# Projections of a two-layer attention trunk: float32r high and low parts replaced by float16 parts with measured power-of-two scales

## The chip, the cores and the metric

The kernel runs on one core of one Trainium2 chip. The metric is the device time of one execution in microseconds (us), given as a median over runs. A core has a matrix engine (PE, with PEld for its loading of stationary tiles), a vector engine (DVE), a scalar engine (ACT), GpSimd (POOL) and SyncE (SP), which in this kernel issues all DMA transfers. Each engine works through a queue of its own in order.

## The reference

A trunk of two layers over 1024 tokens of width 1024, 16 heads of 64. Each layer is a gated mixer:

```python
for i in range(DEPTH):                       # DEPTH = 2
    h = rms_norm(x, norm_g[i])
    if i % 2 == 0: o, gate = fox_mixer(h, ...)            # layer 1
    else:          o, gate = dsw_mixer(h, cos, sin, ...)  # layer 2
    x = x + (o * jax.nn.silu(gate)) @ w_out
# fox_mixer: proj = h @ w_in                       # 4*1024 + 16 columns
#   q, k = rms_norm(per head) * gain;  v, gate, f_logit = the rest
#   c = cumsum(log_sigmoid(f_logit + b_f))
#   o = softmax(q k^T / 8 + c_i - c_j, causal) v
# dsw_mixer: proj = h @ w_in                       # 9*1024 + 1024 columns
#   three groups (window, dilation) = (128,1), (512,4), (2048,16):
#   q, k = partial_rotary(rms_norm(per head) * gain); banded softmax; v
#   o = the three groups' outputs weighted by softmax over their lse
# rms_norm(x, g) = x * rsqrt(mean(x*x) + 1e-6) * g,  all float32
```

## The kernel before, in words

**Precision by pairs.** Each projection is computed from a high and a low part of both operands: `xh`, `xl` for the activations and two halves of `w` for the weights, all float32r. A product takes three matmuls: xh·wh, xh·wl, xl·wh.

**Tiling.** Weights come in blocks of up to 384 columns. `project` (L308, its matmul L313) computes one block for one tile of 128 tokens: eight steps over the contraction, each with three matmuls whose stationary operand is a 128x128 piece of xh or xl and whose moving operand is a slab of the weight. There are 38 such blocks of eight tiles: three for the gates of layer 1 (384, 272 and 384 columns; the middle one carries the forget logits), eight for layer 1's heads, three for the gates of layer 2 (384, 256, 384) and 24 for layer 2 (eight head pairs by three dilation groups). 36 of them have 384 columns. `project_t` (L318, matmul L336) is the output projection at the end of each layer, with the weight stationary and 512 tokens moving.

**Order.** PE is pinned to program order; the order of the other engines is made by a scheduler, from the order in which the program issues its work and from priorities, and each engine then keeps its own order. The program issues work through `Flow`: a slot passes for every six projection matmuls (`flow.tick()` in `project`), so 32 slots to a block, and `flow.at(slot, fn)` puts a piece of work at a slot. While PE does block n, `Weights.ahead` (L294) prepares block n+1 at slots of the table `CFG`:

- `load` (L248): four pairs of slabs, 128x2x384 float32, into two rotating `raw` buffers, at slots 0, 4, 13, 20.
- `bound` (L255, DVE reduce at L258): the largest absolute value of the v columns, for blocks of layer heads only, at slots 9, 14, 22, 27. `scale` (L262) makes from it a power of two for v, at slot 28.
- `split` (L283): for each of eight slabs a copy to float32r on ACT (L289), and the residue by a subtraction (L291), six on POOL and two on DVE.

**Activations.** In layer 1 x arrives transposed from memory (`split_xt`, L521): it is multiplied by the norm's gain and split. It is not divided by the norm; the per-token factor `rx` (L538, `row_factor`) is applied to the results instead, in the gates, in the head norms' epsilon and in v. At the end of layer 1, `grown` (L775) adds the output projection to x, writes x and x times the gain to memory, and gathers squares; `take` (L816) reloads and splits x for layer 2 (L825, L826), and `sums` makes the factors `rx2`. Layer 2's dilated tiles reload x from memory in `reload_x`.

**Around the projections.** In layer 1 (the FoX stage) the scores of head pair n are computed while block n+1 projects. Probabilities are split into float16 halves (`p_transpose`: ACT copy, a subtraction on POOL at L498), transposed by DMA into `ptt`, and multiplied with v at L506 to L508. q and k are transposed by DMA into `qk_t`. Layer 2 (the dilated stage) does likewise with its own subtraction at L912. At the end, `transpose_rows` (L343) turns the gated output y on PE and splits it into xh, xl for `project_t`.

The lines around a split in the program before:

```python
nc.scalar.copy(w[:, 0, :n], raw[:, k % 2, :n])
eng = nc.vector if own or (cfg["wl"][self.layer] >> k) & 1 else nc.gpsimd
eng.tensor_sub(w[:, 1, :n], raw[:, k % 2, :n], w[:, 0, :n].bitcast(F32))
```

Of the kernel before, what the change touches and what calls it, by code (L numbers as in the profile page):

```python
# [82 lines left out]
def trunk(ctx, tc, ins, out, cfg):  # L83
# [42 lines left out]
    ss_d = dram.tile([S], F32, name="ss_d")  # L126
# [16 lines left out]
    xh = const.tile([P, KT, S], F32R, name="xh")  # L143
    xl = const.tile([P, KT, S], F32R, name="xl")
# [81 lines left out]
    gmax = const.tile([P, 2], F32, name="gmax")  # L226

    gmax2 = const.tile([P, 2], F32, name="gmax2")
# [4 lines left out]


# [3 lines left out]
    class Weights:  # L238


        def __init__(self, src, n, vcols=None, layer=0):
            self.src, self.n, self.vcols, self.layer = src, n, vcols, layer
            self.raw, self.slabs, self.vs = {}, [], None
            if vcols is not None:
                self.vm = sm.tile([P, KT // 2], F32, name="vm", tag="vm")
                self.vm2 = sm.tile([P, KT // 2], F32R, name="vm2", tag="vm2")

        def load(self, i, tag=None):  # L248
            if tag is None:
                self.raw[i] = w_p.tile([P, 2, 384], F32, name="raw", tag="raw", bufs=2)  # L250
            else:
                self.raw[i] = lay([P, 2, 384], F32, name="raw", tag=tag)
            nc.sync.dma_start(self.raw[i][:, :, : self.n], self.src[:, 2 * i : 2 * i + 2, :])

        def bound(self, i):  # L255
            if self.vcols is None:
                return
            nc.vector.tensor_reduce(self.vm[:, i : i + 1], self.raw[i][:, :, self.vcols], AX.XY, ALU.max, apply_absolute_value=True)  # L258
            if i == KT // 2 - 1:
                nc.vector.tensor_mul(self.vm2, self.vm, self.vm)  # L260

        def scale(self):  # L262

            if self.vcols is None:
                return

            ws = under["ps"][:, 384 : 384 + KT // 2]
            nc.tensor.matmul(ws, ones, self.vm2, start=True, stop=True)  # L270
            v1 = sm.tile([P, 1], F32, name="v1", tag="v1")
            nc.vector.tensor_reduce(v1, ws, AX.X, ALU.add)
            nc.vector.tensor_scalar(v1, v1, gmax2[:, self.layer : self.layer + 1], None, ALU.mult)

            e = v1.bitcast(I32)
            nc.vector.tensor_scalar(e, e, 1, 0x7FC00000, ALU.logical_shift_right, ALU.bitwise_and)
            nc.vector.tensor_scalar(e, e, float(127 << 22), None, ALU.add)
            nc.vector.tensor_single_scalar(e, e, 0x7F800000, ALU.bitwise_and)
            nc.vector.tensor_scalar(e, e, float(125 << 23), float(154 << 23), ALU.max, ALU.min)
            self.vs = sm.tile([P, 1], F32, name="vs", tag="vs")  # L280
            nc.vector.tensor_scalar(self.vs.bitcast(I32), e, -1.0, float(267 << 23), ALU.mult, ALU.add)

        def split(self, k, own=False):  # L283
            raw, n = self.raw[k // 2], self.n
            if "w2" in layer["bufs"] and k >= KT - 2:
                w = lay([P, 2, 384], F32R, name="w2", tag="w2")
            else:
                w = w_p.tile([P, 2, 384], F32R, name="w", tag="w", bufs=cfg["wbufs"])
            nc.scalar.copy(w[:, 0, :n], raw[:, k % 2, :n])  # L289
            eng = nc.vector if own or (cfg["wl"][self.layer] >> k) & 1 else nc.gpsimd  # L290
            eng.tensor_sub(w[:, 1, :n], raw[:, k % 2, :n], w[:, 0, :n].bitcast(F32))  # L291
            self.slabs.append(w)

        def ahead(self):  # L294

            s0 = flow.now
            for i in range(KT // 2):
                flow.at(s0 + cfg["wload"][i], lambda i=i: self.load(i))
                flow.at(s0 + cfg["wbound"][i], lambda i=i: self.bound(i))
            flow.at(s0 + cfg["wscale"], self.scale)  # L300
            for k in range(KT):
                flow.at(s0 + cfg["wsplit"][k], lambda k=k: self.split(k))
            return self

    def part(src, i, layer=0):
        return Weights(src[i], src[i].shape[2], None, layer)

    def project(w, cols):  # L308
        n = w.n
        ps = under["ps"] = ps_pj.tile([P, 512], F32, name="pj", tag="pj")  # L310
        for k in range(KT):
            for i, (a, j) in enumerate(((xh, 0), (xh, 1), (xl, 0))):
                nc.tensor.matmul(ps[:, :n], a[:, k, cols], w.slabs[k][:, j, :n], start=(k == 0 and i == 0), stop=(k == KT - 1 and i == 2))  # L313
# [4 lines left out]
    def project_t(h, w, done):  # L318


        n = w.n // P
# [8 lines left out]
        for i, (b, m, k) in enumerate(todo):  # L330
# [4 lines left out]
            for x, (j, a) in enumerate(((0, xh), (0, xl), (1, xh))):  # L335
                nc.tensor.matmul(ps[m], w.slabs[k][:, j, m * P : (m + 1) * P], a[:, k, 512 * b : 512 * (b + 1)], start=(k == 0 and x == 0), stop=(k == KT - 1 and x == 2))  # L336
# [6 lines left out]
    def transpose_rows(row, k0, n, t):  # L343
# [4 lines left out]
        dh = xh[:, k0 : k0 + n, t * P : (t + 1) * P]  # L348
        with tc.high_priority(cfg["ph_"]):
            nc.scalar.copy(dh, pv)  # L350
            nc.vector.tensor_sub(xl[:, k0 : k0 + n, t * P : (t + 1) * P], pv, dh.bitcast(F32))
# [9 lines left out]
    def load_gbc(layer):  # L361
        gbc = lay([P, D], F32, name="gbc", tag="ph")
        nc.sync.dma_start(gbc, norm_g[layer].partition_broadcast(P))
        gm = gmax[:, layer : layer + 1]
# [746 lines left out]
```

## Time and profile before

| what | value |
|---|---|
| median of 3 runs | 1812.54 us (1809.61 to 1814.23) |
| span of the profiled execution | 1816.7 us |
| PE busy | 1737.0 us, 96% |
| DVE, ACT, POOL busy | 60%, 56%, 54% |
| DMA traffic | 290.79 MB |

The profiled execution is one of its own, and its span, 1816.7 us, is the only time it has; it lies about 4 us above the median of the timed runs. A matmul's row gives its own duration, and durations overlap: the pace of PE is the distance between starts. The stages by time: first gates to about 143 us, FoX heads to about 600, output projection to about 662, second gates to about 750, dilated heads to about 1720, last output projection to the end.

### The profile page before, as it was taken

How to read it: one execution, taken by the hardware profiler on the slowest of the kernel's cores; microseconds unless marked ns; L12 is line 12 of the kernel's file. 1: busy time of each engine (PE TensorE's matmuls, PEld its weight loads, DVE VectorE, ACT ScalarE, POOL GpSimd, SP SyncE). 2: the span in 40 equal slices, each digit the busy share in tenths (PEclk: the TensorE clock that was granted, in tenths of full speed). 3: DMA queues.
4: the chain of work that ended last, by engine and by line, in shares of the span. 5: the costliest groups of instructions: out<-in, count | busy, mean ns of one | idle time of the engine just before them, and what ended most of it. 6: DMA issues, size and time to landing. Idle time of an engine off the chain costs nothing.

```text
span 1816.7 us, 38150 instructions
## 1 busy us (share of the span) xinstructions
PE 1737.0 (96%) x13276; PEld 1641.7 (90%) x13276; DVE 1093.3 (60%) x3674; ACT 1011.0 (56%) x2696; POOL 973.5 (54%) x1175
## 2 busy tenths in 40 slices
PE   7999999999988989999999999999999999999999
PEld 6999888888876779999999989999999999999877
DVE  8546666666664453365556585666675666667631
ACT  6536666666665465455555665555555555555620
POOL 4215565556545431255656566667576666757530
PEclk9999999999999999999999999999999999999999
DMA  8447999999999763456767687667677776667852
GB/s 285 127 130 140 193 190 185 176 177 183 187 190 207 213 188 114 127 113 134 142 133 144 146 191 143 157 140 152 138 163 144 162 151 143 149 140 179 189 154 85
DMA packets 653189, 290.79 MB, mean 160 GB/s; under 512 B 512306, under 2 KB 616754, under 8 KB 652996
## 3 DMA queue, kind: packets, MB, share of 16 engines
q1 hardware_dynamic: 652996, 288.36, 71.4%
q8 instruction: 104, 1.70, 0.4%
q14 instruction: 89, 0.73, 0.1%
HBM read 126.46 MB, written 37.03 MB: 90 GB/s over the span
## 4 chain that ended last, share of the span: by engine, by line
PE 45%; DMA 12%; DVE 6%; ACT 4%; issue 3%; POOL 3%; SPq 1%; DVEq 0%; POOLq 0%; ACTq 0%
PE pj L313 33%; PE pj L336 7%; DMA raw<-in_w_dsw 5%; PE s L450 2%; DMA qk_t<-hl 2%; DMA ptt<-ph 2%; DMA og_d<-og 1%; POOL hl L425 1%; POOL w L291 1%; DMA cmb<-og_d 1%; DVE w L291 1%; DVE hl L426 1%; DVE u L422 1%; PE ob L506 1%; DVE p L906 1%
## 5 line engine op out<-in xcount | busy, mean ns | idle before, releaser
L313 PE MATMUL pj<-w,xh 128*128 128x384 f32 (+2 forms) x4864 | 1259.6, 341 | 30.2 <-ACT w L289 7.3
L313 PEld LDWEIGHTS pj<-w,xh 128*128 128x128 f32 x4864 | 873.1, 191 | 38.9 <-DVE ge L481 7.8
L313 PE MATMUL pj<-w,xl 128*128 128x384 f32 (+2 forms) x2432 | 817.6, 336 | 0.2 <-DVE xl L530 0.2
L313 PEld LDWEIGHTS pj<-w,xl 128*128 128x128 f32 x2432 | 464.7, 191 | 0.9 <-DVE xl L530 0.9
L291 POOL TENSOR_TENSOR w<-raw,w 128x384 fp32r<-128x384 f32 (+2 forms) x258 | 261.7, 1035 | 233.3 <-ACT w L289 228.8
L498 POOL TENSOR_TENSOR ph<-p,ph 128x512 f16<-128x512 f32 (+3 forms) x176 | 172.9, 999 | 161.9 <-ACT ph L495 160.7
L289 ACT CAST w<-raw 128x384 fp32r<-128x384 f32 (+2 forms) x352 | 162.6, 501 | 114.8 <-PE pj L336 37.4
L425 POOL TENSOR_TENSOR hl<-u,hl 128x512 f16<-128x512 f32 x128 | 151.2, 1181 | 125.0 <-ACT hl L424 124.9
L912 POOL TENSOR_TENSOR ph<-p,ph 128x768 f16<-128x768 f32 (+2 forms) x96 | 155.3, 1618 | 102.9 <-ACT ph L911 102.9
L383 ACT ACTIVATE sq<-pj 128x256 f32<-128x256 f32 x256 | 97.2, 380 | 168.9 <-DVE u L378 167.2
L450 PE MATMUL s<-qk_t 128*128 128x128 f16 (+1 forms) x1504 | 162.0, 248 | 19.2 <-DVE acc L658 10.4
L336 PE MATMUL pj<-xh,w 128*128 128x512 f32 x512 | 170.4, 404 | 2.2 <-ACT p L907 1.1
L258 DVE TENSOR_REDUCE vm<-raw 128x1 f32<-128x256 f32 x128 | 53.6, 419 | 156.2 <-DMA raw<-in_w_dsw 118.6
L506 PEld LDWEIGHTS <-ptt 128*128 128x128 f16 x1136 | 102.9, 98 | 48.8 <-issue 27.5
L389 DVE SCALAR_TENSOR_TENSOR vt<-pj,vsr,vt 128x128 f16<-128x128 f32 x256 | 89.6, 350 | 93.2 <-ACT vt L388 92.8
L450 PEld LDWEIGHTS <-qk_t 128*128 128x128 f16 x1504 | 110.2, 98 | 36.1 <-issue 22.0
L424 ACT CAST hl<-u 128x512 f16<-128x512 f32 x128 | 79.2, 619 | 104.9 <-DVE u L422 88.6
L495 ACT CAST ph<-p 128x512 f16<-128x512 f32 (+3 forms) x176 | 88.9, 537 | 72.7 <-DMA ptt<-ph 72.3
L492 ACT ACTIVATE p<-p,acc 128x512 f32<-128x512 f32 (+2 forms) x192 | 109.0, 609 | 30.6 <-DVE acc L658 27.4
L336 PEld LDWEIGHTS pj<-xh,w 128*128 128x128 f32 x512 | 97.6, 191 | 24.5 <-DVE xr L779 1.5
L378 DVE TENSOR_TENSOR u<-pj,gr 128x256 f32<-128x256 f32 x256 | 106.4, 416 | 18.4 <-PE pj L313 18.3
L907 ACT ACTIVATE p<-p,og 128x128 f32<-128x128 f32 (+1 forms) x256 | 98.1, 441 | 33.6 <-DVE og L906 33.4
(171 smaller groups left out, 2609.4 us busy)
## 6 DMA issues: line engine op xcount, KB each, us to landing
raw<-in_w_dsw SPq DMA_DIRECT2D x96, 384.0 KB, 3.7
raw<-in_w_fox SPq DMA_DIRECT2D x32, 384.0 KB, 3.7
og_d<-og SPq DMA_DIRECT2D x64, 132.0 KB, 3.2
cmb<-og_d SPq DMA_DIRECT2D x64, 132.0 KB, 3.3
bc<-c_d SPq DMA_DIRECT2D x32, 256.0 KB, 3.9
gs_d<-ge SPq DMA_DIRECT2D x32, 192.0 KB, 3.2
xt<-in_xt SPq DMA_DIRECT2D x16, 256.0 KB, 6.1
xrow<-in_x SPq DMA_DIRECT2D x8, 512.0 KB, 6.3
```

Source lines behind the costliest of these rows:

```text
L289: nc.scalar.copy(w[:, 0, :n], raw[:, k % 2, :n])
L291: eng.tensor_sub(w[:, 1, :n], raw[:, k % 2, :n], w[:, 0, :n].bitcast(F32))
L313: nc.tensor.matmul(ps[:, :n], a[:, k, cols], w.slabs[k][:, j, :n], start=(k == 0 and i == 0), stop=(k == KT - 1 and i == 2))
L336: nc.tensor.matmul(ps[m], w.slabs[k][:, j, m * P : (m + 1) * P], a[:, k, 512 * b : 512 * (b + 1)], start=(k == 0 and x == 0), stop=(k == K ...
L378: nc.vector.tensor_mul(u[:, t % 2].rearrange("p (a b) d -> p a b d", a=2), ps[:, : 4 * HD].rearrange("p (a b d) -> p a b d", a=2, b=2), gr ...
L425: nc.gpsimd.tensor_sub(hl[:, :, :4, 1], u, hl[:, :, :4, 0])
L450: nc.tensor.matmul(s[:, c0 : c0 + cnt * P].rearrange("p (c s) -> p c s", c=cnt), qk[:, i, blk], kk[:, j : j + cnt, e], start=(h == 0), sto ...
L492: nc.scalar.activation(p, p, AF.Exp, bias=acc, scale=-1.0)
L498: (nc.gpsimd if pool_l else nc.vector).tensor_sub(ph[:, e, 1, cols], p, ph[:, e, 0, cols])
L506: nc.tensor.matmul(o[:, e, :], hi, vt[:, j, e, HD:], start=(b == 0), stop=False, skip_group_check=True)
L907: nc.scalar.activation(p[:, e], p[:, e], AF.Exp, bias=acc[:, e : e + 1], scale=-1.0)
L912: nc.gpsimd.tensor_sub(ph[:, 1], st["p"], ph[:, 0])
```

## The change

All operands of the projections become float16. So that high and low parts keep their accuracy in float16's range, everything is scaled by powers of two which are found from the data:

- `bound` reduces **all** columns of **every** block (768 elements a pair instead of 256), at slots 8, 10, 12, 15. `scale`, at slot 20, now runs for every block: the squares are summed over partitions by a matmul with ones (`spread_sums`), and the power of two `sw`, the inverse `inv` and, for head blocks, the scaled epsilon, the column factor and v's factor follow in 9 or 13 small DVE operations.
- `split` works on a pair of slabs and comes after `scale`, at slots 21, 23, 25, 27. Pairs 1 and 3: ACT copies with `scale=sw`, and one DVE instruction multiplies and subtracts 768 elements (L301). Pairs 0 and 2: POOL multiplies `raw` in place (L303), ACT copies, POOL subtracts (L305).
- Because nothing can be split before the whole block is measured, `raw` has four buffers instead of two; the loads are at slots 2, 4, 6, 9.
- x is divided by its norm before the split. In layer 1 a diagonal matrix `dg` of the row factors goes through a matmul with ones (L578, `nb`), and DVE multiplies x by it. For layer 2 `factors` does the same with 512 tokens at a time, `take` multiplies, splits and writes the normalised x to `xm_d`, which `reload_x` reads. The factors `rx`, `rx2` and `vsr` at the results are gone; the constants `inv`, `eps` and `vs` of the block are applied in the same instructions.
- y has its own `yh`, `yl` with a scale `sy`, from the largest gate value (a reduction a gate tile into `peak`) and the smallest weight scale.
- At the start, row 0, x tile 0, all four weight pairs and the gains are loaded before anything is split.

```diff
-    xh = const.tile([P, KT, S], F32R, name="xh")
-    xl = const.tile([P, KT, S], F32R, name="xl")
+    xh, xl, yh, yl = (const.tile([P, KT, S], F16, name=n) for n in ("xh", "xl", "yh", "yl"))
...
+    def spread_sums(src, n):
...
+        nc.tensor.matmul(ws, ones.bitcast(src.dtype), src, start=True, stop=True)
+        v1 = sm.tile([P, 1], F32, name="v1", tag="v1")
+        nc.vector.tensor_reduce(v1, ws, AX.X, ALU.add)
+        return v1
...
-            self.raw[i] = w_p.tile([P, 2, 384], F32, name="raw", tag="raw", bufs=2)
+        def load(self, i):
+            self.raw[i] = w_p.tile([P, 2, 384], F32, name="raw", tag="raw", bufs=4)
...
-            nc.vector.tensor_reduce(self.vm[:, i : i + 1], self.raw[i][:, :, self.vcols], AX.XY, ALU.max, apply_absolute_value=True)
+            nc.vector.tensor_reduce(self.vm[:, i : i + 1], self.raw[i][:, :, : self.n], AX.XY, ALU.max, apply_absolute_value=True)
...
+        def split(self, i, own=False):
+            raw, n = self.raw[i][:, :, : self.n], self.n
+            w = self.pairs[i] = w_p.tile([P, 2, 2, 384], F16, name="w", tag="w", bufs=cfg["wbufs"])
+            if own or (cfg["wl"][self.layer] >> i) & 1:
+                nc.scalar.activation(w[:, 0, :, :n], raw, AF.Copy, scale=self.sw)
+                nc.vector.scalar_tensor_tensor(w[:, 1, :, :n], raw, self.sw, w[:, 0, :, :n], ALU.mult, ALU.subtract)
             else:
+                nc.gpsimd.tensor_scalar(raw, raw, self.sw, None, ALU.mult)
+                nc.scalar.copy(w[:, 0, :, :n], raw)
+                nc.gpsimd.tensor_sub(w[:, 1, :, :n], raw, w[:, 0, :, :n])
...
+    def split_xt(t):
+        nb = ps_s.tile([P, 512], F32, name="nb", tag="s")
+        nc.tensor.matmul(nb[:, :P], ones.bitcast(F32), fac.pop(t), start=True, stop=True)
+        for h in range(2):
+            xv = xts.pop((t, h)).rearrange("p (k s) -> p k s", k=4)
+            nc.vector.tensor_mul(xv, xv, nb[:, :P].unsqueeze(1).broadcast_to([P, 4, P]))
+            dh = xh[:, 4 * h : 4 * h + 4, t * P : (t + 1) * P]
+            nc.scalar.copy(dh, xv)
+            (nc.gpsimd if t > 1 and h else nc.vector).tensor_sub(xl[:, 4 * h : 4 * h + 4, t * P : (t + 1) * P], xv, dh)
...
         def split(i):
+            nc.vector.tensor_mul(xs[:, i], xs[:, i], fac2[b])
...
-CFG = dict(... wl=(0x50, 0x50), ... wbufs=12, ... wload=(0, 4, 13, 20), wbound=(9, 14, 22, 27), wscale=28, wsplit=(10, 11, 15, 16, 29, 29, 30, 30))
+CFG = dict(... wl=(0xA, 0xA), ... wbufs=8, ... wload=(2, 4, 6, 9), wbound=(8, 10, 12, 15), wscale=20, wsplit=(21, 23, 25, 27))
```

**Where instructions move.** First the start of PE's queue. Before, PE begins with the projection of tile 0, slab by slab (pj is the result, w the weight pair, the number behind a name the buffer's):

```order
L313 MATMUL pj_217<-w_149,xh_107 128x384 x2
L313 MATMUL pj_217<-w_149,xl_108 128x384
L313 MATMUL pj_217<-w_152,xh_107 128x384 x2
L313 MATMUL pj_217<-w_152,xl_108 128x384
L313 MATMUL pj_217<-w_155,xh_107 128x384 x2
```

After the change, the sum of the weights' squares and the norm matmuls of tiles 0, 1 and 2 (`dg_174`, `dg_224`, `dg_244`) stand ahead of it:

```order
L248 MATMUL ws_184<-vm2_131,ones_125 128x4
L578 MATMUL nb_196<-dg_174,ones_125 128x128
L578 MATMUL nb_228<-dg_224,ones_125 128x128
L578 MATMUL nb_259<-dg_244,ones_125 128x128
L328 LDWEIGHTS xh_107
L328 MATMUL pj_279<-w_204,xh_107 128x384
```

The first projection matmul has moved behind `dg_244`. On DVE, after the change, that diagonal is made at the end of this stretch; `raw_306` is the second pair of slabs of the second block, `gm_725` the second layer's gains:

```order
L270 TENSOR_REDUCE vm_251<-raw_306 128x1
L384 TENSOR_SCALAR gm_725<-gm_725 128x1
L375 SCALAR_TENSOR_TENSOR nv_236<-nv_236 128x1
L374 TENSOR_TENSOR nv_330<-nv_330 128x1
L375 SCALAR_TENSOR_TENSOR nv_267<-nv_267 128x1
L385 TENSOR_SCALAR sx_118<-gm_725 128x1
L376 SCALAR_TENSOR_TENSOR nv_236<-nv_236 128x1
L375 SCALAR_TENSOR_TENSOR nv_330<-nv_330 128x1
L376 SCALAR_TENSOR_TENSOR nv_267<-nv_267 128x1
L552 TENSOR_SCALAR gt2_129<-gt2_129,sx_118 128x8
L570 TENSOR_SCALAR dg_244<-ident_90,nv_236 128x128
```

So the first projection matmul now stands behind reductions of the next block and the small operations of several tiles.

The second place is POOL at the end of a FoX block. Before (ph are split probabilities, hl split q and k, w the weights of the next block):

```order
L498 TENSOR_TENSOR ph_4224<-p_4209,ph_4224 128x512
L425 TENSOR_TENSOR hl_4163<-u_4092,hl_4163 128x2x4x64
L498 TENSOR_TENSOR ph_4224<-p_4216,ph_4224 128x512
L498 TENSOR_TENSOR ph_4285<-p_4270,ph_4285 128x512
L291 TENSOR_TENSOR w_4357<-raw_3899,w_4357 128x384
L498 TENSOR_TENSOR ph_4285<-p_4277,ph_4285 128x512
L291 TENSOR_TENSOR w_4391<-raw_4090,w_4391 128x384
```

After:

```order
L303 TENSOR_SCALAR raw_3612<-raw_3612,ws_f_4174 128x768
L303 TENSOR_SCALAR raw_3754<-raw_3754,ws_f_4174 128x768
L531 TENSOR_TENSOR ph_4152<-p_4144,ph_4152 128x384
L457 TENSOR_TENSOR hl_4041<-u_3906,hl_4041 128x2x4x64
L305 TENSOR_TENSOR w_4220<-raw_3612,w_4220 128x768
L531 TENSOR_TENSOR ph_4321<-p_4306,ph_4321 128x512
L305 TENSOR_TENSOR w_4330<-raw_3754,w_4330 128x768
L531 TENSOR_TENSOR ph_4321<-p_4313,ph_4321 128x512
L531 TENSOR_TENSOR ph_4386<-p_4371,ph_4386 128x512
```

All four of POOL's operations on the weights have moved ahead of the last tile's probabilities (`ph_4386`, the counterpart of `ph_4285`).

The third place is DVE at the handoff from layer 1 to layer 2. Before, the splits of x (L826) stand between the output projection's additions and wait for no factor:

```order
L779 TENSOR_TENSOR xr_9464<-pj_9435,xr_9464 128x512
L826 TENSOR_TENSOR xl_108<-xs_9480,xh_107 128x4x128 x2
L826 TENSOR_TENSOR xl_108<-xs_9491,xh_107 128x4x128 x2
L826 TENSOR_TENSOR xl_108<-xs_9498,xh_107 128x4x128 x2
L779 TENSOR_TENSOR xr_9519<-pj_9476,xr_9519 128x512
```

After, the factor chain (`fv`, `fy`) comes first, then multiplications by `fy`, then the splits:

```order
L374 TENSOR_TENSOR fv_9636<-fy_9637 128x512
L375 SCALAR_TENSOR_TENSOR fv_9636<-fv_9636,fv_9635 128x512
L376 SCALAR_TENSOR_TENSOR fy_9637<-fv_9636,fy_9637 128x512
L860 TENSOR_TENSOR xs_9572<-xs_9572,fy_9637 128x512 x2
L860 TENSOR_TENSOR xs_9583<-xs_9583,fy_9637 128x512 x2
L860 TENSOR_TENSOR xs_9609<-xs_9609,fy_9637 128x512 x2
L301 SCALAR_TENSOR_TENSOR w_9676<-raw_9496,ws_f_9629,w_9676 128x768
L864 TENSOR_TENSOR xl_108<-xs_9572,xh_107 128x4x128
```

The split of x now stands behind the sum of squares, its inverse root and six multiplications.

More of the change, by code (lines that the diff above doesn't have):

```diff
@@ L277, in scale @@
[L277 to L286, printed above, removed]
-            else:
[L288 to L292, printed above, removed]
+            v1 = spread_sums(self.vm2, KT // 2)
@@ L318, in project_t @@
     def project_t(h, w, done):
+        under["ps"] = None
         n = w.n // P
@@ L463, in v_tile, with gates @@
         return vt
-    def gates(src, w, nxt, rows, before=None, after=None):
+    def gates(src, w, nxt, layer, before=None, after=None):
         for h, (c0, n) in enumerate(PARTS):
-            w2 = part(src, h + 1).ahead() if h < 2 else nxt().ahead()
+            w2 = part(src, h + 1, layer, "gate").ahead() if h < 2 else nxt().ahead()
             for t in range(NT):
```

312 lines of the change are left out of this document (169 added, 143 removed).

## The prediction

> **What bounds the kernel now.** I read the page's busy shares, slices and chain first.
>
> ```profile
> PE 1737.0 (96%) x13276; PEld 1641.7 (90%) x13276; DVE 1093.3 (60%) x3674; ACT 1011.0 (56%) x2696; POOL 973.5 (54%) x1175
> PE   7999999999988989999999999999999999999999
> PEclk9999999999999999999999999999999999999999
> PE 45%; DMA 12%; DVE 6%; ACT 4%; issue 3%; POOL 3%; SPq 1%; DVEq 0%; POOLq 0%; ACTq 0%
> ```
>
> PE works nearly everywhere, its clock is granted, and it has by far the largest share of the chain. A dip stands at the start and a shallow one around slices 12 to 15. So a shorter matmul shortens the program wherever its operands come in time, and anything that keeps PE waiting is added in full. The groups by form say which matmuls change:
>
> ```profile
> L313 PE MATMUL pj<-w,xh 128*128 128x384 f32 x4608 | 1213.8, 344 | 28.4 <-ACT w L289 7.3 <-DVE u L422 6.0 <-DVE vt L389 4.8
> L313 PE MATMUL pj<-w,xl 128*128 128x384 f32 x2304 | 781.6, 339 | 0.2 <-DVE xl L530 0.2
> L336 PE MATMUL pj<-xh,w 128*128 128x512 f32 x512 | 170.4, 404 | 2.2 <-ACT p L907 1.1 <-DVE xr L779 1.0
> ```
>
> That is 4608 + 2304 = 6912 matmuls of 384 columns and 512 + 256 = 768 of 512 (the xl group of L336). Their mean durations overlap in the pipeline, so the price of one is the distance between starts, from PE's rows in order of time:
>
> ```profile
> 399.81 0.19 PE L507 MATMUL o<-vt,ptt 128*128 128x64 f16 x1
> ...
> 400.33 1.04 PE L450 MATMUL s<-qk_t 128*128 128x256 f16 x8
> 401.20 0.22 PE L656 MATMUL s<-tri_b,ident_b 128*128 128x128 bf16 x1
> ...
> 401.67 0.34 PE L313 MATMUL pj<-w,xl 128*128 128x384 f32 x1
> ...
> 403.24 0.33 PE L313 MATMUL pj<-w,xl 128*128 128x384 f32 x1
> ...
> 619.52 0.39 PE L336 MATMUL pj<-xl,w 128*128 128x512 f32 x1
> ...
> 622.95 0.39 PE L336 MATMUL pj<-xl,w 128*128 128x512 f32 x1
> ```
>
> Nine float32r matmuls of 384 columns lie between 401.67 and 403.24: 174.4 ns each. Fifteen of 512 between 619.52 and 622.95: 228.7 ns. In float16, 17 of 64 or 65 columns start between 399.81 and 400.33, 30.6 ns each, and eight of 256 take 0.87 us, 108.8 ns each. The slope between those two is 0.409 ns a column, so I estimate 161.1 ns at 384, 213.5 at 512 and 115.3 at 272.
>
> **The matmuls.** 6912 x (174.4 - 161.1) = 92 us, 768 x (228.7 - 213.5) = 12 us, and the 192 of 272 columns (126.9 ns on float32r's own slope) give 2: **-105 us**. All of it lies on PE's path, about 2.6 us a weight block (192 x 13.3 ns), as long as the others keep pace. Bounds of this term: 0, if float16 ran as float32r does, and 105.
>
> The Trainium skill ("TensorE: Matmul & The Clock Gate", "Wait — 56ns, not 53.3ns?") puts a warm matmul at N / 2.4 GHz plus about 2.5 ns, which is 162.5 ns at 384 and 215.8 at 512. It agrees with the 108.8 ns at 256 columns (109.2 by it) and would make this term -94 and the time 11 us more than mine.
>
> **The start.** PE starts early now:
>
> ```profile
> 7.28 1.28 PE L313 MATMUL pj<-w,xh 128*128 128x384 f32 x2 [7.28 <-ACT w L289]
> ...
> 26.11 1.01 PE L313 MATMUL pj<-w,xh 128*128 128x384 f32 x2 [3.02 <-DVE ge L481]
> GB/s 0 179 232 296 313 391 412 414 392 391 370 396 408 314 356 385 400 413 383 393 377 356 193 198 244 107 114 5 70 61 131 44 0 82 119 375 221 6 90 301
> L530 DVE TENSOR_TENSOR xl<-xt,xh 128x512 fp32r<-128x512 f32 x16 | 12.8, 808 | 0.8 <-ACT xh L529 0.7
> L524 DVE TENSOR_TENSOR xt<-xt,gt 128x512 f32<-128x512 f32 x10 | 7.9, 798 | 1.2 <-DMA gt<-in_norm_gt 1.2
> L291 DVE TENSOR_TENSOR w<-raw,w 128x384 fp32r<-128x384 f32 x8 | 4.2, 554 | 1.4 <-ACT w L289 1.4
> L543 DVE TENSOR_SCALAR rx<-nv 128x1 f32<-128x1 f32 x8 | 1.2, 150 | 0.1
> L258 DVE TENSOR_REDUCE vm<-raw 128x1 f32<-128x256 f32 x128 | 53.6, 419 | 156.2 <-DMA raw<-in_w_dsw 118.6 <-DMA raw<-in_w_fox 37.0
> L396 DVE TENSOR_REDUCE pj<-sq 128x8 f32<-128x512 f32 x128 | 88.3, 690 | 45.0 <-ACT sq L383 45.0
> ```
>
> Now no weight may be split before all four pairs are measured. Row 0, the gains, x tile 0 and the four pairs are 3.1 MB; at the rates above (1.5 us a bin) the last lands at about 11.5 us. A reduction costs 0.419 us at 256 columns and 0.690 at 512, so 0.96 at 768 and 1.2 at 1024; the sum over partitions takes half a us more (estimate, it is a matmul and back): 13 us. Then the order of the queues decides, not the first tile's data. PE issues the norm matmuls of tiles 0, 1 and 2 ahead of its first projection, and the third needs DVE's diagonal of tile 2, which stands far down. Ahead of it DVE has, from 13 us on: four multiplications of x (0.80), four subtractions (0.81), four weight residues of 768 (2 x 0.554), the reduction of the second layer's gains (1.2), two of the next block's slabs of 544 (0.73), their kin of 0.5, and 33 one-column operations at 0.15 to 0.2: 3.2 + 3.2 + 4.4 + 1.2 + 1.5 + 0.5 + 5.6 = 19.6 us. So the first projection starts near **32 us** (26 to 38: without the idle fractions, or with DMA waits in between) where it was 7.28. Of the 25 us lost, the first block returns up to 5, the wait of 3.0 at least, since its weights and three x tiles are then ready: **+20** (12 to 30).
>
> **The FoX stage.** Here the DMA engines are nearly full, and POOL feeds the transposed probabilities that PE waits for:
>
> ```profile
> 196.00:251.00 55.00, 51.20 (x510) 47.62 (x509) 36.00 (x130) 35.09 (x88) 33.06 (x33) 1.00 0.98 186
> PE o L506 <- DMA ptt<-ph: 13.2, 10, 2.9
> L912 POOL TENSOR_TENSOR ph<-p,ph 128x768 f16<-128x768 f32 x40 | 66.5, 1662 | 41.6 <-ACT ph L911 41.6
> L527 POOL CAST xh<-xt 128x512 fp32r<-128x512 f32 x6 | 5.6, 940 | 0.4
> L291 POOL TENSOR_TENSOR w<-raw,w 128x384 fp32r<-128x384 f32 x234 | 242.0, 1055 | 205.3 <-ACT w L289 200.7 <-DVE zt L595 2.8 <-PE pj L313 1.5
> ```
>
> The row of 55 us (PE, PEld, DVE, ACT, POOL busy, clock, DMA share, GB/s) is a whole block, its DMA engines 98% busy. POOL's work per block hardly changes: six subtractions of 1.055 (6.3 us) become two scalings and two subtractions. No POOL operation with a factor per partition is in the trace; the nearest row is the one-input cast, 0.940 at 512, so 1.41 at 768 (bounds: 1.0, the 384-column subtraction, and 1.66, the two-input one at 768). With 1.66 for each subtraction that is 6.1 us. But it comes in one lump: all four now stand ahead of the last tile's probabilities, where one of 1.05 stood and a second one behind, 4.0 us more if both are counted, and SP issues all four weight loads ahead of the last tile's transposes. I take 1.75 us a block on the path, near the 13.2 / 7 = 1.9 of today's wait: 8 x 1.75 = **+14** (-5, if the shorter DMA traffic in the second half of a block gives today's waits back, to 30, if all 4.0 are exposed).
>
> **The handoff.** x of layer 2 was split as it came; now it waits for its norm factor, sixteen multiplications of 512 are added on DVE, and the normalised x is written out again.
>
> ```profile
> L826 DVE TENSOR_TENSOR xl<-xs,xh 128x512 fp32r<-128x512 f32 x16 | 17.3, 1127 | 13.7 <-ACT xh L825 13.6
> ```
>
> At 1.13 us each the multiplications are 18 us. The first half of the tokens is finished under the output projection's second half, the last half is needed by the gates' fifth tile, so half is exposed at most: **+8** (0 to 18).
>
> **The dilated stage.**
>
> ```profile
> 1400.00:1490.00 90.00, 87.20 (x647) 84.96 (x646) 59.30 (x223) 50.95 (x155) 62.97 (x88) 1.00 0.70 160
> L291 DVE TENSOR_TENSOR w<-raw,w 128x384 fp32r<-128x384 f32 x18 | 19.8, 1101 | 0.1
> PE pj L313 <- DVE u L422: 6.0, 7, 1.6
> PE pj L313 <- DVE vt L389: 4.8, 4, 2.6
> ```
>
> A block is 40 us here (36 of the reductions in the 360 us from 1220 to 1580, four to a block), DVE busy for 59.30 / 90 x 40 = 26.4. The change gives it four reductions of 0.96 for 0.419 (+2.2), six more small operations (+1.0), and two residues of 768 for two of 384. The old residue costs 1.101 here and 0.554 at the start, where POOL is quiet; the new one is 1.1 to 2.2, I take 1.8 (+1.4). That is 31.0 us in a block of 37.4, 83% for 66%. The waits on DVE are 10.8 us now; scaled by busy over idle (4.9 for 1.95) they become 27: **+16** (0, if they are chance alignments, to 40, if DVE paces half the blocks). ACT loses 8 casts of 0.5 for 4 of 0.8 and the row-factor copies: nothing. The narrow gate additions (a reduction of 0.55 a tile) lie beside 4 us of matmuls: nothing.
>
> **Sum.** -105 + 20 + 14 + 8 + 16 = -47 on the profiled 1816.7, so 1770; the median is 0.9977 of that span: **1766**. With the terms' bounds, most of them not at one end together, 1735 to 1800.
>
> **Rivals.** (1) *Cover holds.* Slack in the buffers and the early loads hide the POOL lump and DVE's load: only start and handoff stay, -77, 1736. For it: PE waits for POOL's w just rarely. Against: DMA at 98%. Chance 0.18. (2) *DVE becomes the bound of the dilated stage.* If its queue fills each time a reduction, a residue and a pair of heads meet, the 24 blocks stay at 40 us and their 61 us of gain is replaced by the 16 I charged: about 1810, down to 1795 if a quarter escapes. 83% busy on average speaks against, the contended 1.101 for. Chance 0.10. (3) *Slower: POOL's scaling by a factor is dear.* If it costs c, 16 of them in FoX lie ahead of the transposes and add 16 x (c - 1.41); the gain is gone at c = 4.3, and at 5 the time is 1823. No row excludes it, the one-input cast speaks against. Chance 0.08. (4) *Float16 streams no faster than float32r at 384 columns*: 1870. The 256-column row speaks against. Chance 0.03. The forecast keeps 0.61.
>
> **How the numbers follow.** A difference under 0.3% (5.4 us) cannot be told from none. Faster: forecast 0.59 of its 0.61, rival 1 and two thirds of rival 2: 0.84. Same: 0.05, from rival 2 and the forecast's edge. Slower: rivals 3 and 4: 0.11. Eight in ten lie in 1724 to 1810: below, rival 1 with the start's lower bound; above, all of rival 2.
>
> **What would show it.** Start distances of 161 to 163 ns at 384 columns; the first projection at 32 us behind a matmul of L578; a PE wait at L506's successor on ptt near 27 us in FoX; POOL's scaling near 1.4 and DVE's residue near 1.8 us; DVE about 83% in the dilated stage. I am wrong if the waits do not grow (rival 1) or if a dilated block still takes 40 us.

## The result and the profile after

The changed kernel takes **1935.68 us** (median; 1927.23 to 1936.61), the kernel before 1813.28 beside it: a ratio of 1.067 (95% interval 1.064 to 1.069), **slower** where 1766 was forecast. Its profiled execution spans 1934.7 us, 118.0 more than before's 1816.7. The page of the changed kernel (busy time and share of the span; granted clock in 40 slices; the chain that ended last):

```profile
PE 1688.3 (87%) x13308; PEld 1071.8 (55%) x13308; DVE 1318.4 (68%) x4089; ACT 1010.9 (52%) x2492; POOL 1081.7 (56%) x1105
...
PEclk9999999988989998999999999999999999999999
...
PE 25%; DMA 17%; DVE 15%; issue 5%; ACT 5%; POOL 4%; SPq 1%; DVEq 0%; ACTq 0%; POOLq 0%
```

PE's share of the chain fell from 45% to 25%; DMA and DVE took it. No engine is busier than 87%. PE is busy for 48.7 us less than before and idle for 166.7 us more, so what was added is waiting; but 48.7 is also less than half of the 105 us that the shorter matmuls were to save. Where PE runs without waits the matmuls became faster, as forecast. PE in order of time (changed kernel):

```profile
989.76 0.33 PE L328 MATMUL pj<-w,xl 128*128 128x384 f16 x1
...
996.58 0.33 PE L328 MATMUL pj<-w,xl 128*128 128x384 f16 x1
```

42 float16 matmuls of 384 columns in 6.82 us are 162.4 ns each, where float32r took 174.4. What the parts beside them cost (groups by form; count, busy us and mean ns; idle time before them):

```profile
L303 POOL TENSOR_SCALAR raw<-raw,ws_f 128x768 f32<-128x768 f32 x78 | 171.5, 2208 | 109.5 <-DVE ws_f L282 109.5
L305 POOL TENSOR_TENSOR w<-raw,w 128x768 f16<-128x768 f32 x78 | 138.1, 1774 | 2.6 <-ACT w L304 2.6
L270 DVE TENSOR_REDUCE vm<-raw 128x1 f32<-128x768 f32 x160 | 150.9, 945 | 96.7 <-DMA raw<-in_w_dsw 71.1 <-DMA raw<-in_w_fox 11.9 <-DMA raw<-in_w_gate 6.1
L301 DVE SCALAR_TENSOR_TENSOR w<-raw,ws_f,w 128x768 f16<-128x768 f32 x82 | 114.3, 1396 | 28.5 <-ACT w L300 28.5
```

The reduction (0.945) and the subtraction (1.774) are near the charged 0.96 and 1.66, DVE's residue (1.396) is below the charged 1.8. POOL's scaling is 2.208 where 1.41 was charged, dearer than the two-input subtraction.

**Where the time went.** The starts of PE's weight blocks cut both programs into the same stages (us; the forecast's terms are put into them by the number of their matmuls):

| stage | before | after | difference | forecast |
|---|---|---|---|---|
| to the second head block of layer 1 (three gate blocks, one head block) | 143.8 | 164.2 | +20.4 | +10 |
| six FoX blocks | 324.0 | 361.8 | +37.8 | -5 |
| last head block, rest of attention, output projection | 191.8 | 193.5 | +1.7 | -5 |
| gates of layer 2 | 99.9 | 106.0 | +6.1 | +2 |
| 24 dilated blocks | 957.6 | 1010.4 | +52.8 | -45 |
| rest | 99.7 | 98.8 | -0.9 | -6 |

Two stages hold 91 of the 118 us. PE's waits in them, FoX first (164 to 526 us, then 825 to 1836; total, times, longest):

```profile
PE o L539 <- DMA ptt<-ph: 33.4, 11, 5.4
PE s L482 <- DMA qk_t<-hl: 24.7, 6, 6.9
...
PE s L482 <- DMA qk_t<-hl: 53.4, 22, 5.1
PE pj L328 <- DVE vt L421: 42.8, 23, 3.5
```

Before, the same stages showed 10.8 us on ptt, none on qk_t in FoX and 2.4 on it later, and 4.8 on vt. The windows of both kernels (busy of PE, PEld, DVE, ACT, POOL; clock; DMA share; GB/s), before first:

```profile
143.00:468.00 325.00, 305.80 (x2990) 285.22 (x2989) 210.72 (x753) 209.72 (x529) 192.06 (x191) 0.99 0.94 182
759.00:1717.00 958.00, 940.67 (x7134) 917.56 (x7133) 618.49 (x2229) 546.11 (x1595) 605.72 (x801) 1.00 0.71 150
```

```profile
164.00:526.00 362.00, 303.48 (x2982) 209.81 (x2982) 243.56 (x794) 212.59 (x498) 207.34 (x180) 0.92 0.81 164
825.00:1836.00 1011.00, 909.42 (x7139) 580.79 (x7137) 702.70 (x2393) 537.30 (x1477) 658.22 (x752) 0.96 0.66 143
```

FoX was at a DMA share of 0.94 before and is at 0.81 now: its DMA engines have room, and PE waits all the same. PE's busy time fell by 2.3 us in FoX and 31.3 in the dilated stage, where about 15 and 61 were forecast for the matmuls. Part of what is missing is the clock that PE was granted: it fell from 0.99 to 0.92 and from 1.00 to 0.96 (the last section shows such a stretch). DVE is busy 702.70 of 1011 us in the dilated stage, 70%, not the 83% of the forecast, and still PE waits for it.

**What such a wait looks like.** DVE of the changed kernel in a dilated block (start, duration, what ended the idle time before), then PE:

```profile
1407.16 0.95 DVE L270 TENSOR_REDUCE vm<-raw 128x1 f32<-128x768 f32 x1 [1.13 <-DMA raw<-in_w_dsw]
1408.04 2.13 DVE L301 SCALAR_TENSOR_TENSOR w<-raw,ws_f,w 128x768 f16<-128x768 f32 x1
1410.09 0.34 DVE L421 SCALAR_TENSOR_TENSOR vt<-pj,ws_f,vt 128x128 f16<-128x128 f32 x1
...
1418.30 0.95 DVE L270 TENSOR_REDUCE vm<-raw 128x1 f32<-128x768 f32 x1 [2.08 <-DMA raw<-in_w_dsw]
1419.17 0.28 DVE L458 COPY hl<-hl 128x512 f16<-128x512 f16 x1
```

```profile
1410.48 0.48 PE L328 MATMUL pj<-w,xh 128*128 128x384 f16 x2 [1.89 <-DVE vt L421]
...
1423.35 1.46 PE L482 MATMUL s<-qk_t 128*128 128x128 f16 x8 [4.36 <-DMA qk_t<-hl]
```

DVE's queue is in order. A reduction waits there for a weight load that has not landed, with a short operation behind it that PE needs: L421, which frees a projection's result (behind L301 too, 2.13 us), and L458, without which q and k cannot be transposed; POOL had its part of `hl` ready at 1414.46, nearly 5 us before L458 ran. PE then waits 1.89 and 4.36 us. The kernel before has the same pattern, with shorter reductions (DVE, kernel before):

```profile
1412.07 0.42 DVE L258 TENSOR_REDUCE vm<-raw 128x1 f32<-128x256 f32 x1 [1.51 <-DMA raw<-in_w_dsw]
1412.41 0.34 DVE L389 SCALAR_TENSOR_TENSOR vt<-pj,vsr,vt 128x128 f16<-128x128 f32 x1
```

There PE waited 4.8 us in all for vt, so the pattern alone does not give the price. And at a FoX block's border, POOL:

```profile
327.51 4.39 POOL L303 TENSOR_SCALAR raw<-raw,ws_f 128x768 f32<-128x768 f32 x2
331.86 1.39 POOL L531 TENSOR_TENSOR ph<-p,ph 128x384 f16<-128x384 f32 x1
333.21 1.15 POOL L457 TENSOR_TENSOR hl<-u,hl 128x512 f16<-128x512 f32 x1
334.32 1.63 POOL L305 TENSOR_TENSOR w<-raw,w 128x768 f16<-128x768 f32 x1
335.92 1.20 POOL L531 TENSOR_TENSOR ph<-p,ph 128x512 f16<-128x512 f32 x1
337.08 1.64 POOL L305 TENSOR_TENSOR w<-raw,w 128x768 f16<-128x768 f32 x1
```

Two scalings in a row, 4.39 us, with probabilities and hl behind them and the rest of the split between. The next block's loads, whose buffers this frees, are then issued on SP ahead of the transposition of those probabilities:

```profile
337.66 2.23 SPq L267 DMA_DIRECT2D raw<-in_w_fox  x2
...
342.37 0.38 SPq L267 DMA_DIRECT2D raw<-in_w_fox  x1
342.86 4.08 SPq L532 DMA_TRANSPOSE ptt<-ph  x1
```

### The profile page after: what moved, and what is told of

Its sections match the earlier page's. It is cut to its first block, busy times and chain, and to the rows that moved or that the text cites. A ratio compares the mean times of both kernels' runs of the same rounds, so it can differ in the third digit from the quotient of the medians.

```text
span 1934.7 us, 38039 instructions
## 1 busy us (share of the span) xinstructions
PE 1688.3 (87%) x13308; PEld 1071.8 (55%) x13308; DVE 1318.4 (68%) x4089; ACT 1010.9 (52%) x2492; POOL 1081.7 (56%) x1105
## 4 chain that ended last, share of the span: by engine, by line
PE 25%; DMA 17%; DVE 15%; issue 5%; ACT 5%; POOL 4%; SPq 1%; DVEq 0%; ACTq 0%; POOLq 0%
PE pj L328 17%; DMA qk_t<-hl 6%; DMA raw<-in_w_dsw 6%; PE pj L352 5%; DVE w L301 3%; DMA ptt<-ph 2%; PE s L482 2%; DVE vm L270 2%; DVE p L943 1%; DMA og_d<-og 1%; ACT p L944 1%; DVE pj L428 1%; DVE u L410 1%; DMA raw<-in_w_do 1%; DVE u L454 1%
## 5 line engine op out<-in xcount | busy, mean ns | idle before, releaser
L328 PE MATMUL pj<-w,xh 128*128 128x384 f16 (+2 forms) x4864 | 1212.9, 334 | 55.5 <-DVE vt L421 43.3
L328 PE MATMUL pj<-w,xl 128*128 128x384 f16 (+2 forms) x2432 | 809.8, 333 | 9.2 <-DVE xl L864 7.8
L328 PEld LDWEIGHTS <-xh 128*128 128x128 f16 x4864 | 480.4, 101 | 353.6 <-issue 90.0
L328 PEld LDWEIGHTS <-xl 128*128 128x128 f16 x2432 | 244.4, 101 | 180.8 <-issue 23.7
L303 POOL TENSOR_SCALAR raw<-raw,ws_f 128x768 f32<-128x768 f32 (+2 forms) x86 | 184.2, 2151 | 116.1 <-DVE ws_f L282 113.2
L482 PE MATMUL s<-qk_t 128*128 128x128 f16 (+1 forms) x1504 | 168.2, 255 | 91.6 <-DMA qk_t<-hl 82.8
L270 DVE TENSOR_REDUCE vm<-raw 128x1 f32<-128x768 f32 (+2 forms) x176 | 161.7, 921 | 100.1 <-DMA raw<-in_w_dsw 71.1
L352 PE MATMUL pj<-yh,w 128*128 128x512 f16 x512 | 161.8, 386 | 1.0 <-POOL w L305 1.0
L305 POOL TENSOR_TENSOR w<-raw,w 128x768 f16<-128x768 f32 (+2 forms) x86 | 148.3, 1729 | 4.2 <-ACT w L304 4.2
L301 DVE SCALAR_TENSOR_TENSOR w<-raw,ws_f,w 128x768 f16<-128x768 f32 (+2 forms) x90 | 121.6, 1353 | 33.4 <-ACT w L300 33.4
L421 DVE SCALAR_TENSOR_TENSOR vt<-pj,ws_f,vt 128x128 f16<-128x128 f32 x256 | 89.1, 348 | 59.1 <-ACT vt L420 58.0
```

Of the source, the lines that this page charges most:

```text
L301: nc.vector.scalar_tensor_tensor(w[:, 1, :, :n], raw, self.sw, w[:, 0, :, :n], ALU.mult, ALU.subtract)
L303: nc.gpsimd.tensor_scalar(raw, raw, self.sw, None, ALU.mult)
L305: nc.gpsimd.tensor_sub(w[:, 1, :, :n], raw, w[:, 0, :, :n])
L328: nc.tensor.matmul(ps[:, :n], a[:, k, cols], w.slab(k, j), start=(k == 0 and i == 0), stop=(k == KT - 1 and i == 2))
L352: nc.tensor.matmul(ps[m], w.slab(k, j)[:, m * P : (m + 1) * P], a[:, k, 512 * b : 512 * (b + 1)], start=(k == 0 and x == 0), stop=(k == KT ...
L482: nc.tensor.matmul(s[:, c0 : c0 + cnt * P].rearrange("p (c s) -> p c s", c=cnt), qk[:, i, blk], kk[:, j : j + cnt, e], start=(h == 0), sto ...
```

## The experiments

Three theories were put to the test. **A, the price**: POOL's dear scaling. **B, the ring**: weight loads wait for raw buffers, and SP's and DVE's queues wait behind them. **C, the measuring**: either its work on DVE, or the dependence that it creates (nothing can be split before the last pair of a block is measured). Times are medians; the ratio is to the kernel before, which runs at 1813 to 1818 beside them. Here is all of it by the stages that matter (profiled executions, us). The table counts six FoX and 24 dilated blocks, as above; the expectations count one FoX block more and one dilated block fewer, which for the change is 396.5 and 963.4 us.

| kernel | time | ratio (95%) | six FoX blocks | 24 dilated blocks |
|---|---|---|---|---|
| before | 1813.3 | 1 | 324.0 | 957.6 |
| the change | 1935.7 | 1.067 (1.064 to 1.069) | 361.8 | 1010.4 |
| act_scale | 1902.2 | 1.048 (1.045 to 1.051) | 362.6 | 968.9 |
| raw6 | 1927.1 | 1.061 (1.058 to 1.065) | 363.1 | 1002.8 |
| late_loads | 1920.2 | 1.058 (1.055 to 1.062) | 362.4 | 992.6 |
| fixed_scale | 1831.2 | 1.008 (1.006 to 1.011) | 322.3 | 963.3 |
| measured_unused | 1928.2 | 1.062 (1.058 to 1.066) | 327.5 | 1033.1 |
| narrow_measure | 1911.2 | 1.053 (1.051 to 1.055) | 360.1 | 989.0 |
| early_split | 1899.0 | 1.045 (1.043 to 1.047) | 365.5 | 969.5 |
| fixed_act | 1800.3 | 0.990 (0.988 to 0.993) | 314.3 | 928.4 |
| early_act_start | 1884.2 | 1.038 (1.035 to 1.041) | 350.4 | 974.5 |
| fixed_act_spread | 1798.4 | 0.991 (0.988 to 0.994) | 320.5 | 930.4 |
| act_measure | 1893.6 | 1.042 (1.040 to 1.045) | 359.2 | 966.7 |
| act_measure_early | 1875.0 | 1.032 (1.030 to 1.034) | 356.5 | 957.6 |

**act_scale.** The scaling of pairs 0 and 2 on ACT.

```diff
-                nc.gpsimd.tensor_scalar(raw, raw, self.sw, None, ALU.mult)
+                nc.scalar.activation(raw, raw, AF.Copy, scale=self.sw)
```

> One edit: the in-place scaling of the raw weight pairs 0 and 2 goes from POOL to ACT (ACT multiplies by sw in place, then casts; POOL only subtracts). Theory A, the price: POOL's scaling takes 2.15 us where 1.41 was charged, and two of them in a row at the end of a block hold up the splits of q, k and probabilities behind them on POOL, so the transposed qk_t (82.8 us of PE's waits) and ptt (34.1) come late. A expects both waits to fall by more than half and the time near 1850. Theory B, the ring: weight loads wait for raw buffers that the last splits free, and SP's and DVE's queues stand behind them. B expects at most 20 us, near 1915, and the 43 us that PE waits for vt unchanged.

It gains 33 us. The dilated stage gains 41.5 (1010.4 to 968.9), and the gates of layer 2 and the last output projection lose some of it. In FoX, where A had put the harm, the time is the same; one wait took the place of another (PE's waits of act_scale from 164 to 527 us):

```profile
PE s L482 <- DMA qk_t<-hl: 31.1, 6, 7.5
PE pj L328 <- DVE vt L421: 18.3, 7, 4.8
PE s L482 <- DVE acc L707: 8.9, 10, 1.3
PE o L539 <- DMA ptt<-ph: 3.7, 3, 2.5
```

ptt fell from 33.4 to 3.7 us, vt rose from 0.5 to 18.3. A holds for the dilated stage alone.

**raw6 and late_loads.** Six raw buffers for four (and seven w pairs for eight); loads and reductions at later slots.

```diff
-tag="raw", bufs=4)   ... wbufs=8
+tag="raw", bufs=6)   ... wbufs=7
```

> raw has six buffers instead of four, paid for by one w pair fewer (seven instead of eight). B, the ring: with two buffers to spare the first two loads of a block no longer wait for the end of the splits before them; DVE's 83 us of waiting for raw in its reductions and PE's waits for vt (43 us) fall by half, qk_t's too, time near 1870. A, the price: POOL's lump is as it was, time within 10 us of 1936. A third reading, C, that measuring all columns itself is what DVE cannot carry, expects no change either.

```diff
-wload=(2, 4, 6, 9), wbound=(8, 10, 12, 15)
+wload=(7, 9, 11, 13), wbound=(14, 15, 17, 18)
```

> Loads of the next weights at slots 7, 9, 11, 13 instead of 2, 4, 6, 9 and reductions at 14, 15, 17, 18 instead of 8, 10, 12, 15; buffers unchanged. B in the form that SP's queue is the harm (loads that wait for raw stand ahead of the transposes): loads come when raw is long free, the waits on qk_t and ptt at block starts go, time near 1880. B in the form that DVE's reductions are the harm: vt's 43 us go too, since the data are there when the reductions come up. A: 1936 within 10.

Both gain little (9 and 15 us) and nothing in FoX. In raw6 PE's wait for vt falls from 43.3 to 1.2 us, as B expected, but qk_t rises from 82.8 to 99.9 and u (L454) from 1.1 to 11.4 over the program: taking one wait away showed the next. B in this form falls as the main cause.

**fixed_scale.** No measuring of weights: a constant in place of the measured root (its kernel leaves the weights' reductions and their sum out).

```diff
-            nc.vector.tensor_reduce(self.vm[:, i : i + 1], self.raw[i][:, :, : self.n], ...)
...
-            v1 = spread_sums(self.vm2, KT // 2)
-            e = v1.bitcast(I32)
-            root_floor(e, e, -16, 40)
+            e = two.bitcast(I32)
```

> Leaves out the measuring of the weights: no reduction over the weights, no sum over partitions, the power of two is a constant (2.0 in place of the measured root), the rest of the small operations and all slots of loads and splits stay. C, the measuring: DVE loses 162 us of reductions with their 83 us of waits for raw; PE's waits for vt (43) and most of qk_t (83) go, time near 1830. A: POOL's lump stays at the block's end, time above 1900.

1831 as C expected: measuring is worth 104 of the 122 us. FoX falls by 39.5 us and the dilated stage by 47.

**measured_unused and narrow_measure** part C's two halves: all the work without the dependence, and the dependence with little of the work.

```diff
 # measured_unused: fixed_scale, and the measuring is put back with its result unused
+            unused = spread_sums(self.vm2, KT // 2).bitcast(I32)
+            root_floor(unused, unused, -16, 40)
             e = two.bitcast(I32)
 # narrow_measure: the change, but
-self.raw[i][:, :, : self.n]
+self.raw[i][:, :, :4]
```

> As fixed_scale (the weights are scaled by a constant, so the scale is not the measured one), but all reductions, the sum over partitions and the root are done as in the change and their result is not used: the work of measuring without the dependence of the split on it. If DVE's work and its queue's waits for raw are the cost, the time goes back to 1900 or more; if the dependence (nothing can be split before the last pair is measured, and all splits fall in the last slots) is the cost, it stays near fixed_scale's 1831, below 1855.

> The reductions read only the first 4 columns of each slab (8 numbers a pair instead of 768; the rest of the weights is not measured), everything else as in the change: the dependence without most of the work. DVE loses some 130 of 162 us of reductions, keeps its waits for raw. If the dependence is the cost: near 1910 or above. If DVE's work is the cost: below 1870.

By the totals neither half alone is the cause; the stages tell them apart. **In FoX it is the dependence**: with all the work but no dependence of the split on the scale the six blocks take 327.5 us, with the dependence and hardly any work 360.1. **In the dilated stage it is the reductions in DVE's queue**: narrow ones give back 21 of the 47 us that leaving out the measuring gave (a narrow one still waits there for its load), and act_measure below, which keeps the dependence and takes them off DVE, gives back 44. Without the dependence the stage is even slower (1033.1); why is open. What the missing dependence moves in FoX is seen on POOL of measured_unused, whose block starts at 274.1:

```profile
283.88 2.21 POOL L305 TENSOR_SCALAR raw<-raw,ws_f 128x768 f32<-128x768 f32 x1 [2.24 <-DVE vm L272]
286.05 2.82 POOL L533 TENSOR_TENSOR ph<-p,ph 128x512 f16<-128x512 f32 x3
288.83 1.15 POOL L459 TENSOR_TENSOR hl<-u,hl 128x512 f16<-128x512 f32 x1
290.30 2.21 POOL L305 TENSOR_SCALAR raw<-raw,ws_f 128x768 f32<-128x768 f32 x1 [0.32 <-DVE vm L272]
```

The scalings come one by one early in the block, each behind the reduction of its own pair (`<-DVE vm`; it overwrites what the reduction reads, so this much dependence stays), and only the subtractions stay at its end; in the change all of it sits at the border.

**early_split.** The split spread over the block.

```diff
-wload=(2, 4, 6, 9), wbound=(8, 10, 12, 15), wscale=20, wsplit=(21, 23, 25, 27)
+wload=(0, 1, 2, 4), wbound=(4, 6, 8, 10), wscale=12, wsplit=(13, 17, 21, 25)
```

> Measuring and splitting spread over the block: loads at slots 0, 1, 2, 4, reductions at 4, 6, 8, 10, scale at 12, splits at 13, 17, 21, 25 (there are buffers for two whole blocks of w). If the lump at the block's end is the cost, the waits on ptt (34) and qk_t (83) fall by half and the time is near 1870. If DVE's work is the cost, it stays within 15 us of 1936.

41 us in the dilated stage, none in FoX. There the two scalings still came in a row (4.4 us in the middle of the block) and PE still waited for ptt and qk_t. So it is not the border alone: in the middle of the block a lump that hangs on one scale cost FoX as much.

**fixed_act.** fixed_scale and act_scale together.

> As fixed_scale (weights not measured, a constant scale), and the scaling of pairs 0 and 2 on ACT as in act_scale. If the two costs add, 1831 - 33 = 1798; if POOL's lump mattered only behind the measuring, near 1831.

They add: 1800.3, 1.0% faster than before (0.988 to 0.993). It leaves the measuring of the weights out, so it serves only weights of a magnitude known in advance. Its FoX blocks (window of fixed_act):

```profile
200.00:480.00 280.00, 253.43 (x2623) 176.25 (x2624) 181.88 (x620) 188.16 (x443) 160.62 (x148) 0.97 0.95 189
```

With PE's new pace and few waits FoX has the DMA share of before, 0.95, and 314.3 us for 324.0. That is consistent with DMA being the limit there, which would let FoX keep 10 of the 15 us that its six blocks' matmuls save: PE's busy time over the six blocks is 289.0 us, 15 less than before, and PE waits 19.7 us for ptt, where it was 10.8. No run tests the DMA engines alone.

**early_act_start and fixed_act_spread** put edits together, and test the start: x tile t + 2 is prepared behind the projection of tile t.

```diff
+                pg = project(w, tile_cols(0, t))
                 if h == 0 and before is not None:
                     before(t)
-                pg = project(w, tile_cols(0, t))
```

> The change with the measuring kept whole, and three edits together: slots as in early_split, POOL's scaling on ACT as in act_scale, and in the first gates the preparation of x tile t+2 issued behind the projection of tile t instead of ahead of it. If the dilated stage's two gains add (45 us by act_scale, 40 by early_split), that stage takes about 880 us; FoX, which neither edit moved by more than 2 us, stays at 395 if the dependence itself is the cost there and falls below 380 if only POOL and the splits' place were; the first projection starts near 20 us (DVE's row of tile 2's diagonal no longer stands ahead) where it was 32.3, and some 10 us are gained. Together near 1840, at best 1815.

> Weights not measured, a constant scale, as in fixed_act (1800); besides, loads at slots 0, 4, 13, 20 and splits at 10, 15, 20, 26, and x tile t+2 prepared behind the projection of tile t. If lumps of loads and splits at the block's border still cost something without the dependence, FoX falls from 347 to about 335 and the dilated stage from 886 to about 870; the start gains 10. Near 1765; if the order of the splits does not matter any more, 1790.

The first projection of early_act_start starts at 20.5 us instead of 32.3, as worked out, and nothing is gained: its first block ends at 79.3 us, against 71.1 in the change and 76.7 in early_split, which has the same early slots. PE waits later, for work on DVE (rows of early_act_start):

```profile
27.99 0.34 PE L328 MATMUL pj<-w,xl 128*128 128x384 f16 x1 [1.27 <-DVE xl L584]
34.88 0.80 PE L578 MATMUL nb<-dg,ones 128*128 128x128 f32 x2 [3.98 <-DVE dg L570]
```

The dilated gains of act_scale and early_split do not add (974.5 together, 968.9 and 969.5 alone), and FoX gains 11. Without the measuring the order of loads and splits makes no difference to the total (1798 for 1800), though FoX takes 320.5 us for 314.3.

**act_measure and act_measure_early.** The measuring on ACT, as a sum of squares instead of the largest value (a larger bound and so a smaller scale); the second with early slots and ACT's scaling.

```diff
-            nc.vector.tensor_reduce(self.vm[:, i : i + 1], self.raw[i][:, :, : self.n], AX.XY, ALU.max, ...)
+            nc.scalar.activation(junk[:, :, : self.n], self.raw[i][:, :, : self.n], AF.Square, accum_out=self.vm[:, i : i + 1])
```

> Measuring goes from DVE to ACT with the dependence kept: instead of the largest value DVE takes, ACT squares each pair and sums it (a larger bound, so the scale is smaller by some powers of two); all slots, POOL's scaling and splits as in the change. If DVE's reductions and the waits for raw in DVE's queue are the dilated stage's cost beside POOL's scaling, PE's waits for vt (43) nearly vanish and that stage falls from 963 to 920 to 940, as with narrow_measure, while FoX stays near 395, since the dependence is there as before: near 1895. If the dependence is also the dilated stage's cost, 1930.

> act_measure with the early slots of early_split and POOL's scaling on ACT: every cost that the runs found is off DVE and POOL, only the dependence stays. If DVE's reductions were what kept act_scale and early_split from adding up (dilated stage 923 instead of 880 together), that stage now falls to about 890; FoX near 383 as with those two. Near 1850. If ACT, with squares and scalings some 67% busy, is the next bound, 1880.

act_measure came out as expected: 1893.6, the dilated stage at 966.7, FoX unmoved, PE's wait for vt from 43.3 to 12.9 us. In the second, the 23 dilated blocks of the expectation take 911.4 us, not 890, and the whole 1875: the best version that measures the weights, 3.2% slower than before. **Open** is why three different remedies (POOL's scaling, the early slots, DVE's reductions) each bring the dilated stage to about 968 and together only to 957.6, where fixed_act has 928.4. Open too is by which buffers the dependence holds FoX up: no version that keeps it brings the six blocks under 350 us. That measuring two blocks ahead would free FoX was not tried.

## Why the prediction was wrong

- **What bounds the kernel: right for the kernel before, wrong as a premise.** That "a shorter matmul shortens the program wherever its operands come in time" holds, but "All of it lies on PE's path" was taken to hold in FoX too, whose DMA share of 0.98 stood in the prediction's own row. Freed of the measuring, FoX kept at most 10 of 15 us. And "anything that keeps PE waiting is added in full" was too little: a wait also slowed the matmuls behind it.
- **The matmuls: right in the price of one, not in the sum.** 162.4 ns at 384 columns for the estimated 161.1. The rule of the Trainium skill ("TensorE: Matmul & The Clock Gate", "Wait — 56ns, not 53.3ns?") gives 162.5, and the trace agrees. At the measured 162.4 the 6912 matmuls save 83 us and not 92. But this price holds between waits. PE's busy time fell by 48.7 us and not by 105, and the mean granted clock of the execution fell from 0.990 to 0.953: over its span that is at most 73 us of full-speed time more than before (estimate from the two clocks and spans; some of it fell on waits). The prediction had no term for it.
- **The start: right in place, low in size.** The first projection starts at 32.3 us (forecast 32), behind the diagonal of tile 2:

```profile
31.74 0.80 PE L578 MATMUL nb<-dg,ones 128*128 128x128 f32 x2 [11.22 <-DVE dg L570]
32.32 0.85 PE L328 MATMUL pj<-w,xh 128*128 128x384 f16 x2
```

  The stage lost 20.4 us where 10 were forecast, so the term is about 30, not 20. In early_act_start the first projection came 12 us earlier and the stage was no shorter, so the place of tile 2's diagonal is not the reason; its rows name DVE's work, which no run takes away.
- **The FoX stage: the step that failed first.** "I take 1.75 us a block on the path" counted the work ahead of one instruction. The six blocks lost 37.8 us and should have gained 15: near 9 us a block, more than the 4.0 of work that was moved. What moved was the whole chain, load, measure, scale and split, into one lump that hangs on one scale. measured_unused shows that it is the dependence, not the size of the work. When act_scale took POOL's scaling away, the wait on ptt went and waits on qk_t and vt took its place; through which buffers the delay is handed on is not shown.
- **The dilated stage: the step that failed most.** "That is 31.0 us in a block of 37.4, 83% for 66%", with waits scaled by busy over idle, gave +16. DVE is 70% busy and the block is 42.1 us (1010.4 / 24). Busy share was the wrong measure: DVE's operations wait in order, reductions among them for loads. The stage came out 98 us above its forecast of -45. Leaving out the measuring gives back 47 us, taking the scaling off POOL 41.5, for which this term had nothing at all; both together give 82 (fixed_act, 928.4). In the kernel before, L258 had 156.2 us of idle time ahead of it, more than the 96.7 of L270 after, and an operation that PE needs could stand behind it too; why it cost PE so little there is not shown.
- **POOL's scaling: mis-sized, and charged in one stage only.** 1.41 charged, 2.208 measured, outside the bounds of 1.0 to 1.66. Moving it to ACT gives 33 us back in all. It was rival 3's mechanism, at a price below its threshold of 4.3 and in the other stage.
- **The handoff: right within its bounds.** +6.1 us for the stage, +2 forecast, so the term is about 12 where 8 (0 to 18) was charged.
- **The rivals.** None had measuring's dependence as its mechanism. Rival 2 (DVE binds the dilated stage) named the right engine but held that a block could not get worse than today's 40 us.

## What to carry to other kernels

A value that must be known before any of a block's work can begin turns a spread-out preparation into a lump; its price is what queues behind the lump on every engine. Doing the work without using its result, read stage by stage, can tell whether the dependence or the work is the cost: it did in FoX, and in the dilated stage it took a second experiment. An in-order queue is not judged by its busy share alone: before adding an operation that waits for a load, look for the first instruction behind it that the bounding engine needs. In a stage whose DMA engines are already at 0.94, faster matmuls may not bring all that they save: here 10 of 15 us, once the waits were gone.

## What the runs showed of the hardware

POOL's scaling by a factor per partition, one float32 input, took 2.208 us at 128x768, longer than its two-input subtraction of the same size (1.774, and 1.634 in the FoX stage). ACT did the same scaling in 0.927 (act_scale).

A wait of PE can cost more than its length: here the matmuls after it are slow for a while. The changed kernel after a wait in FoX:

```profile
353.40 1.25 PE L482 MATMUL s<-qk_t 128*128 128x256 f16 x6 [3.51 <-DMA qk_t<-hl]
...
354.55 0.85 PE L328 MATMUL pj<-w,xh 128*128 128x384 f16 x2
...
356.46 0.49 PE L328 MATMUL pj<-w,xh 128*128 128x384 f16 x2
356.79 0.33 PE L328 MATMUL pj<-w,xl 128*128 128x384 f16 x1
356.95 0.49 PE L328 MATMUL pj<-w,xh 128*128 128x384 f16 x2
```

Six matmuls from 354.55 to 356.46 take 318 ns each, the three from 356.46 to 356.95 take 163. The granted clock is 0.50 from 353.03 to 356.44 us and 1.00 from 356.50 to 359.00. By the stage it is 0.92 in FoX for 0.99 before and 0.96 in the dilated stage for 1.00. This is one part of the miss: over such stretches the matmuls do not run at the pace that the prediction multiplied.
